# A scheduler's table of matmul durations is changed, and with it the order of 7,588 TensorE instructions

## The chip, the cores and the metric

One core of a Trainium2 chip runs the whole program. The time is device microseconds (us) of one execution. The kernel before took 1705.38, 1706.32 and 1707.93 us in three runs; the median is 1706.32 us. The profile is of one more execution, with a span of 1705.8 us from the first to the last instruction.

## The reference

Two transformer blocks on 512 tokens of width 1024, all in float32:

```python
h = h + hybrid_mixer(rmsnorm(h, mix_norm), ...)           # state-space scan, causal conv, multi-scale pool
h = h + memory_cross_attention(rmsnorm(h, xattn_norm), rmsnorm(mem, mem_norm), ...)
h = h + swiglu(rmsnorm(h, ffn_norm), ...)
x = rmsnorm(h, final_norm)
# layer A
u, qm, gate = split_cols(x @ a_w_in, A_SIZES)             # u: 2 x 1536 channels
y_mix = conformer_conv(u, conv_w, conv_b, g, b)           # a * sigmoid(gl), 31 taps, layer norm, silu
y = concatenate([y_mix, mem_cross_attention(qm, mem_n, w_mkv)]) * silu(gate)
x = layer_norm(ALPHA * x + y @ w_out, pg, pb)
# layer B: the same frame with dsa_attention (12 heads, top-k keys by an index) in place of the conv
```

## The kernel before

**Layout and products.** Activations lie as tiles of 128 channels by 512 tokens. Each weight block (128 x 1024, 512 KB) comes by one DMA into a tile `raw`; ScalarE (ACT) rounds it to a high part `whi` and VectorE (DVE) takes the rest as `wlo` (`prep`, lines 445 to 455). Activations are split the same way. A product is then three matmuls of the short float type (`mm3`, line 457): high by high, high by low, low by high. The first two need only `whi`; the third needs `wlo`. A `dense` unit for one output tile is 8 x 3 = 24 matmuls of 512 columns into one PSUM bank of the group `mm`, of which there are three. A bank is opened by a unit's first matmul and is free again when DVE or ACT has read it. There are also two banks `A`, two `B` and one `C`.

**Order of the work.** The functions do not issue instructions. Every call is recorded (`Program.rec`, line 137) with its engine, its dependencies and an estimated duration `o.dur`. `Program.order` (line 233) then plays a list schedule with these durations, the latencies between engines of a table, and the slots of tiles and banks, and takes for each free engine the ready instruction of the smallest priority. `Program.emit` (line 359) does this once by program order and up to 12 times more (`FBI`) with priorities from a backward pass (`latest`, line 196), keeps the order with the shortest planned end, and issues all instructions in it. So each engine's queue is fixed at build time: on the chip an instruction waits behind all that stand ahead of it on its engine. All instructions carry the line 378 of `emit`; one tells them apart by tiles.

**Layer A, which the prediction speaks of most.** `conv_tile(j)`, j = 0 to 11 (lines 1134 to 1162), makes the gate half with 24 matmuls of `a_gl` (tanh on ACT), then the other half with 24 of `a_a`; one DVE instruction writes their product into the padded tile `pad` (line 1141). Of the 31 taps ACT and GpSimd (POOL) do 11 into an `act` tile, TensorE does one into a bank `B` (a matmul in full float32, tiles `pad,act`, line 1156), and DVE does 19 more on that bank, one `SCALAR_TENSOR_TENSOR B<-pad,vec,B` each (line 1160). A last DVE addition joins the two sums and `lnc.add` collects the layer norm's statistics. Woven between the conv tiles (line 1203) are the memory attention (`score`, `trans`, `out`, with `emit_y` on DVE after it), the 16 gate tiles (24 matmuls each), and `out_tile`s over the four memory heads. After the twelve tiles come `k_proj` for layer B (line 1206: four units of 24 matmuls of 256 columns), `lnc.finish` (line 1207: 4 + 4 statistics matmuls of one column on `C`, a power on POOL, two broadcasts from `ident,rn` and `ident,rq`), and for each of 12 tiles: two DVE instructions, silu on ACT, the product with the gate on POOL, a split on ACT and DVE (lines 1208 to 1213), whose results the eight `out_tile`s over 12 row tiles read (line 1216).

Of the kernel before, what the change touches and what calls it, by code (L numbers as in the profile page):

```python
# [18 lines left out]
T = 512  # L19
# [11 lines left out]
SSD = 600  # L31
# [27 lines left out]
class View:  # L59
    """a lazily resolved access pattern of a tile"""  # L60
# [61 lines left out]
class Program:  # L122
    """records instructions in program order, then orders each engine's by a list schedule"""
# [13 lines left out]
    def rec(s, eng, fn, m, args, kw):  # L137
        o = Op()
# [25 lines left out]
        n = int(np.prod(out.shape[1:]))  # L164
        if eng == "PE":
            one = m == "transpose" or args[1].base.dt == F32R
            o.table = n > 8
            o.dur = n / 2.4 * 2 if m == "transpose" else max(107, n / 2.4) + 2.5 if one else max(27, n / 2.4) * 4
        elif eng == "ACT":
            ptr = sum(isinstance(kw.get(k), View) for k in ("scale", "bias", "accum_out"))  # L170
            o.dur = n * 0.833 + 93 + 93 * ptr - 40 * (isinstance(args[1], View) and args[1].base.psum)
            o.table = _TABLE.get(args[2])
        elif eng == "DVE":
            two = m in ("tensor_tensor", "scalar_tensor_tensor")
            psum = any(x.psum for x in o.tiles)
            wide = [x for x in ins if int(np.prod(x.shape[1:])) > 1]
            ptr = len(ins) - len(wide)
            if m == "reciprocal":
                o.dur = n * 8.3 + 60
            elif m in ("tensor_reduce", "max", "match_replace"):  # L180
                o.dur = int(np.prod(wide[-1].shape[1:])) * 1.042 + 68
            elif not two and not psum:
                o.dur, o.port = n * 0.521 + 68 + 61 * ptr, n > 8
            else:
                o.dur = n * 1.042 + 68 + 61 * min(ptr, 1)
                o.port = two and sum(not x.base.psum for x in wide) == 2 and n > 8
        elif eng == "POOL":
            o.dur, o.port = (958 if kw.get("op") == ALU.pow else n * (2.2 if len(ins) > 1 else 1.0) + 99), n > 8
        else:
            o.dur = n * int(out.shape[0]) * 4 / 360.0  # L190
# [5 lines left out]
    def latest(s, prio):  # L196
        """latest starts, from a list schedule of the reversed program"""
# [8 lines left out]
        while events:  # L206
# [4 lines left out]
            for e, q in ready.items():  # L211
                if busy[e] > now or not q:
                    continue
                o = ops[q[0][1]]
# [18 lines left out]
    def order(s, prio, window):  # L233
# [3 lines left out]
        left, first, last = {}, {}, {}  # L237
# [5 lines left out]
        # slots in use if the rest ran in program order: a tile may take one early only if this never exceeds the number there is  # L243
# [8 lines left out]
        early, wait, back = [], [], deque()  # L252
# [9 lines left out]
        while len(seq) < len(ops):  # L262
# [5 lines left out]
            while fin and fin[0][0] <= now:  # L268
                o = ops[heapq.heappop(fin)[1]]
# [10 lines left out]
            while back and back[0][0] <= now:  # L280
                x = back.popleft()[1]
# [99 lines left out]
def body(ctx, tc, t, out):  # L381
# [141 lines left out]
    class LN:  # L523
        """layer norm over tiles that come one by one, centred first by the mean of the first npil tiles, whose sum is then 0"""
# [29 lines left out]
        def finish(s):  # L554
            """broadcast rows r, q with norm = centred * r - q"""
# [36 lines left out]
    # ================= block 1, mixer =================  # L592
# [27 lines left out]
    # time steps of all heads  # L620
# [30 lines left out]
    # softplus(x) = max(x, 0) + log1p(exp(-|x|)), log1p(e) = 2 atanh(e / (2 + e))  # L651
# [20 lines left out]
    # cumulated steps as rows of heads  # L672
# [16 lines left out]
    # causal convolution of xs, B, C; order of the channel tiles: B0 B1 C0 C1, then xs  # L689
# [15 lines left out]
    # z gate  # L705
# [7 lines left out]
    # B in token rows, B C products  # L713
# [85 lines left out]
    # multi-scale pool  # L799
# [58 lines left out]
    # keys and values of the first memory  # L858
# [76 lines left out]
    # normalised SSD branch  # L935
# [12 lines left out]
    # ================= block 1, cross attention =================  # L948
# [3 lines left out]
    class XAttn:  # L952
        """two heads (2 pr, 2 pr + 1) of 4; q: nd tiles [dims, T] per head; scale(tb): a number or a column per token"""
# [57 lines left out]
    def weave(*lists):  # L1011
        """emits the lists of steps in turns, each spread evenly over the longest"""
        n = max(len(x) for x in lists)
        pos = [0] * len(lists)
        for i in range(n):
            for k, x in enumerate(lists):
                want = -(-(i + 1) * len(x) // n)
                while pos[k] < want:
                    x[pos[k]]()
                    pos[k] += 1  # L1020
# [9 lines left out]
    q = []  # L1030
# [23 lines left out]
    # ================= block 1, swiglu =================  # L1054
# [25 lines left out]
    # taps of layer A: sigmoid(x) = (1 + tanh(x / 2)) / 2, and the half goes to the taps; some as diagonal matrices  # L1080
# [40 lines left out]
    # ================= final norm of block 1 =================  # L1121
# [8 lines left out]
    # ================= block 2, layer A =================  # L1130
# [40 lines left out]
    def gate_tile(w, j, half=False):  # L1171
        """silu(gate); with half, twice that from tanh"""
# [14 lines left out]
    def out_tile(w, j, part, first, ln=None):  # L1187
        """part: the operands by row tile"""
# [37 lines left out]
    # ================= block 2, layer B =================  # L1226
# [103 lines left out]
    # token rows for the last layer norm  # L1330
# [50 lines left out]
    # last projection, token rows  # L1381
# [152 lines left out]
```

## Time and profile before

| | |
|---|---|
| timed runs | 1705.38, 1706.32, 1707.93 us; median 1706.32 |
| the profiled execution's own time | span 1705.8 us (0.5 us under the median; no other time of it is shown) |
| TensorE (PE) | 1665.2 us busy, 98%, 7966 records |
| VectorE (DVE) | 1142.2 us, 67% |
| ScalarE (ACT) | 775.9 us, 45% |
| GpSimd (POOL) | 421.0 us, 25% |
| DMA | mean 92 GB/s |

PE's busy time counts a matmul until its result is out, about 0.39 us for one of 512 columns, while the next starts long before; so the start-to-start spacing tells what a matmul costs in a dense row. A matmul in full float32 shows as two records, a transpose as one: 6912 short-float matmuls, 378 in full float32 and 298 transposes make the 7966 records. The 40 slices of the page show where PE is not full.

### The profile page before, as it was taken

How to read it: one execution, taken by the hardware profiler on the slowest of the kernel's cores; microseconds unless marked ns; L12 is line 12 of the kernel's file. 1: busy time of each engine (PE TensorE's matmuls, PEld its weight loads, DVE VectorE, ACT ScalarE, POOL GpSimd, SP SyncE). 2: the span in 40 equal slices, each digit the busy share in tenths (PEclk: the TensorE clock that was granted, in tenths of full speed). 3: DMA queues.
4: the chain of work that ended last, by engine and by line, in shares of the span. 5: the costliest groups of instructions: out<-in, count | busy, mean ns of one | idle time of the engine just before them, and what ended most of it. 6: DMA issues, size and time to landing. Idle time of an engine off the chain costs nothing. (4 is left out here: it accounts for less than half of the span.)

```text
span 1705.8 us, 21241 instructions
## 1 busy us (share of the span) xinstructions
PE 1665.2 (98%) x7966; PEld 1361.4 (80%) x7966; DVE 1142.2 (67%) x1801; ACT 775.9 (45%) x1349; POOL 421.0 (25%) x325
## 2 busy tenths in 40 slices
PE   9999999999999999999999997999899999999998
PEld 7888678888888888888878775778787788788886
DVE  7836778574565435544477999988747895467754
ACT  6722444444553222332356766545435434545541
POOL 1004433020031001201233678965630000000000
PEclk9999999999999999999999998999999999999999
DMA  7321212531242333322323311232233123211121
GB/s 242 117 86 56 93 50 87 160 99 50 75 131 93 98 99 99 95 79 90 117 91 108 102 56 50 81 127 87 75 124 115 62 99 94 80 63 50 53 84 50
DMA packets 49719, 156.32 MB, mean 92 GB/s; under 512 B 5648, under 2 KB 7568, under 8 KB 49616
## 3 DMA queue, kind: packets, MB, share of 16 engines
q1 hardware_dynamic: 49616, 154.96, 28.2%
q8 instruction: 63, 1.03, 0.3%
q14 instruction: 40, 0.33, 0.1%
HBM read 152.71 MB, written 2.10 MB: 91 GB/s over the span
## 5 line engine op out<-in xcount | busy, mean ns | idle before, releaser
L378 PE MATMUL mm<-act,whi 128*128 128x512 f32 (+1 forms) x3888 | 1194.3, 388 | 18.5 <-DVE act L378 12.9
L378 PEld LDWEIGHTS mm<-act,whi 128*128 128x128 f32 x3888 | 717.8, 189 | 174.3 <-ACT act L378 15.3
L378 PE MATMUL mm<-act,wlo 128*128 128x512 f32 (+1 forms) x1944 | 749.4, 388 | 9.8 <-DVE wlo L378 9.6
L378 ACT ACTIVATE whi<-raw 128x1024 fp32r<-128x1024 f32 (+3 forms) x293 | 289.4, 991 | 582.0 <-PE mm L378 352.5
L378 POOL TENSOR_TENSOR act<-act,act 128x512 f32<-128x512 f32 (+1 forms) x252 | 372.5, 1493 | 683.7 <-DVE act L378 314.8
L378 DVE TENSOR_TENSOR wlo<-raw,whi 128x1024 fp32r<-128x1024 f32 (+3 forms) x293 | 373.2, 1281 | 123.7 <-ACT whi L378 118.9
L378 PEld LDWEIGHTS mm<-act,wlo 128*128 128x128 f32 x1944 | 366.9, 189 | 85.5 <-DVE wlo L378 11.3
L378 DVE TENSOR_TENSOR act<-mm,act 128x512 f32<-128x512 f32 (+3 forms) x173 | 114.6, 664 | 244.9 <-PE mm L378 236.9
L378 ACT ACTIVATE act<-act 128x512 f32<-128x512 f32 (+2 forms) x222 | 134.7, 617 | 104.6 <-DVE act L378 65.9
L378 DVE SCALAR_TENSOR_TENSOR B<-pad,vec,B 128x512 f32<-128x512 f32 x228 | 167.2, 753 | 5.7 <-PE B L378 1.5
L378 DVE TENSOR_TENSOR act<-act,act 128x512 f32<-128x512 f32 (+3 forms) x203 | 138.3, 711 | 26.2 <-ACT act L378 25.3
L378 POOL TENSOR_TENSOR fr<-fv,mhalf 128x1 f32<-128x1 f32 x4 | 2.2, 547 | 410.5 <-DVE fv L378 410.5
L378 ACT ACTIVATE act<-pad,vec 128x512 f32<-128x512 f32 x144 | 94.8, 730 | 11.6 <-DVE pad L378 11.4
L378 PE MATMUL A<-act,act 128*128 128x256 f32 (+6 forms) x488 | 97.8, 342 | 0.3
L378 PEld LDWEIGHTS A<-act,act 128*128 128x128 f32 (+1 forms) x488 | 72.1, 189 | 16.7 <-issue 5.6
L378 PE MATMUL mm<-whi,act 128*128 128x512 f32 x264 | 85.0, 393 | 0.0
L378 ACT ACTIVATE act<-C 128x128 f32<-128x128 f32 (+4 forms) x164 | 52.2, 359 | 70.6 <-PE C L378 68.3
L378 PE MATMUL B<-act,act 128*128 128x128 f32 (+2 forms) x492 | 71.0, 284 | 0.0
L378 PEld LDWEIGHTS B<-act,act 128*128 128x128 f32 (+1 forms) x492 | 61.7, 167 | 9.6 <-issue 3.4
L378 ACT ACTIVATE act<-mm 128x512 f32<-128x512 f32 (+3 forms) x92 | 51.7, 566 | 18.4 <-PE mm L378 18.3
L378 PEld LDWEIGHTS mm<-whi,act 128*128 128x128 f32 x264 | 49.4, 188 | 9.6
L378 PE MATMUL mm<-wlo,act 128*128 128x512 f32 x132 | 51.8, 393 | 0.0
(130 smaller groups left out, 965.6 us busy)
## 6 DMA issues: line engine op xcount, KB each, us to landing
raw<-in_w_g_dram SPq DMA_DIRECT2D x22, 512.0 KB, 3.3
raw<-in_w_u_dram SPq DMA_DIRECT2D x22, 512.0 KB, 3.3
raw<-in_w_om_dram SPq DMA_DIRECT2D x16, 512.0 KB, 3.8
raw<-in_w_d_dram SPq DMA_DIRECT2D x16, 512.0 KB, 3.5
raw<-in_a_gate_dram SPq DMA_DIRECT2D x16, 512.0 KB, 3.4
raw<-in_b_gate_dram SPq DMA_DIRECT2D x16, 512.0 KB, 3.3
raw<-in_b_wo_dram SPq DMA_DIRECT2D x16, 512.0 KB, 3.3
raw<-in_w_xbc_dram SPq DMA_DIRECT2D x12, 512.0 KB, 4.2
```

What stands on the lines that cost most here:

```text
L378: r = o.fn(*[real(a) for a in o.args], **{k: real(v) for k, v in o.kw.items()})
```

## The change

The expression for the planned duration of a PE instruction is another one. `n` is the number of columns, `one` a short-float matmul; the last case is full float32.

```diff
-            o.dur = n / 2.4 * 2 if m == "transpose" else max(107, n / 2.4) + 2.5 if one else max(27, n / 2.4) * 4
+            o.dur = 108.0 if m == "transpose" else max(112.0, n / 2.4 + 14) if one else 2 * max(111.0, n / 1.2 + 2)
```

In ns: a short-float matmul of 512 columns goes from 215.8 to 227.3, of 256 from 109.5 to 120.7; a transpose of 128 from 106.7 to 108; a full float32 matmul of 512 from 853 to 857, of 128 from 213 to 222, of one column from 108 to 222. The rest of the diff takes comments and docstrings out. The instructions, their operands and the number of tiles and banks are the same; the order that `order` and `latest` make of them is not. ACT's function tables, which follow from its order, are loaded 9 times in place of 11. Three places of the new order follow; numbers in names are buffer numbers and differ between the two programs.

**Place 1: conv tile 8, PE and DVE.** The row of PE just ahead of the first low-part matmul of conv tile 8's gate half (the last row of each piece), before:

```order
L378 MATMUL A_8359<-act_8012,act_7315 128x512
L378 MATMUL mm_8369<-act_6810,whi_8313 128x512
L378 MATMUL B_8371<-pad_7986,act_4671 128x512
L378 MATMUL mm_8369<-act_6827,whi_8313 128x512
L378 MATMUL mm_8382<-act_8052,whi_8341 128x512
L378 MATMUL mm_8382<-act_8114,whi_8341 128x512
L378 MATMUL A_8359<-act_8015,act_7658 128x512
L378 MATMUL A_8393<-act_8017,act_7315 128x512
L378 MATMUL A_8393<-act_8022,act_7658 128x512
L378 MATMUL mm_8336<-act_6810,wlo_8439 128x512
```

and after:

```order
L378 MATMUL mm_8339<-act_8078,whi_8200 128x512
L378 MATMUL mm_8346<-act_8024,whi_8282 128x512
L378 MATMUL mm_8346<-act_8078,whi_8282 128x512
L378 MATMUL C_8382<-ident,act_7672 128x128 x4
L378 MATMUL C_8403<-ident,act_7726 128x128 x4
L378 MATMUL C_8416<-ident,act_8008 128x128 x4
L378 MATMUL A_8426<-act_8370,act_7186 128x512
L378 MATMUL A_8426<-act_8372,act_7447 128x512
L378 MATMUL A_8445<-act_8376,act_7186 128x512
L378 MATMUL A_8445<-act_8378,act_7447 128x512
L378 MATMUL mm_8308<-act_6808,wlo_8456 128x512
```

From the end of conv tile 7's second half to that row stand 11 short-float matmuls of 512, 5 full float32 ones and 4 transposes before, and 8, 7 and 14 after. On DVE the low part that this row reads, `wlo_8439`, follows these instructions before:

```order
L378 SCALAR_TENSOR_TENSOR B_8261<-pad_7775,vec_73,B_8261 128x512
L378 SCALAR_TENSOR_TENSOR B_8371<-pad_7986,vec_73,B_8371 128x512
L378 SCALAR_TENSOR_TENSOR B_8261<-pad_7775,vec_73,B_8261 128x512
L378 SCALAR_TENSOR_TENSOR B_8371<-pad_7986,vec_73,B_8371 128x512
L378 TENSOR_TENSOR wlo_8439<-raw_8153,whi_8233 128x1024
L378 TENSOR_TENSOR wlo_8441<-raw_8248,whi_8313 128x1024
```

and after, as `wlo_8456`:

```order
L378 TENSOR_TENSOR act_8211<-act_8211,B_8214 128x512
L378 SCALAR_TENSOR_TENSOR B_8331<-pad_7975,vec_73,B_8331 128x512
L378 SCALAR_TENSOR_TENSOR act_8440<-A_8313,act_7723 128x512
L378 SCALAR_TENSOR_TENSOR B_8331<-pad_7975,vec_73,B_8331 128x512
L378 SCALAR_TENSOR_TENSOR act_8448<-A_8426,act_7998 128x512
L378 SCALAR_TENSOR_TENSOR B_8331<-pad_7975,vec_73,B_8331 128x512 x2
L378 TENSOR_TENSOR wlo_8456<-raw_8116,whi_8179 128x1024
```

Between the instruction that writes conv tile 7's `pad` and this low part, DVE has 20 instructions before and 30 after: 25 taps in place of 19, two joins and two `emit_y` more.

**Place 2: the last two conv tiles, DVE.** From the `pad` of conv tile 10 (first row) to the `pad` of tile 11, before:

```order
L378 SCALAR_TENSOR_TENSOR pad_8470<-act_9025,mm_8972 128x512
L378 TENSOR_TENSOR wlo_9072<-raw_8995,whi_9058 128x1024
L378 SCALAR_TENSOR_TENSOR B_9077<-pad_8470,vec_73,B_9077 128x512 x11
L378 TENSOR_TENSOR act_8750<-act_8750,B_8767 128x512
L378 SCALAR_TENSOR_TENSOR B_9077<-pad_8470,vec_73,B_9077 128x512 x8
L378 TENSOR_TENSOR wlo_9224<-raw_9032,whi_9123 128x1024
L378 TENSOR_TENSOR wlo_9232<-raw_9044,whi_9167 128x1024
L378 TENSOR_TENSOR wlo_9241<-raw_9083,whi_9206 128x1024
L378 SCALAR_TENSOR_TENSOR pad_8592<-act_9131,mm_9140 128x512
```

and after, with the rows behind it:

```order
L378 SCALAR_TENSOR_TENSOR pad_8434<-act_9055,mm_9063 128x512
L378 TENSOR_TENSOR wlo_9119<-raw_9021,whi_9108 128x1024
L378 SCALAR_TENSOR_TENSOR B_9121<-pad_8434,vec_73,B_9121 128x512 x12
L378 TENSOR_TENSOR wlo_9212<-raw_9079,whi_9189 128x1024
L378 SCALAR_TENSOR_TENSOR pad_8526<-act_9172,mm_9169 128x512
L378 SCALAR_TENSOR_TENSOR B_9121<-pad_8434,vec_73,B_9121 128x512
L378 TENSOR_TENSOR wlo_9234<-raw_9088,whi_9214 128x1024
L378 SCALAR_TENSOR_TENSOR B_9232<-pad_8526,vec_73,B_9232 128x512
L378 SCALAR_TENSOR_TENSOR B_9121<-pad_8434,vec_73,B_9121 128x512
L378 SCALAR_TENSOR_TENSOR B_9232<-pad_8526,vec_73,B_9232 128x512
```

Tile 11's `pad` comes after 14 instructions in place of 24, and the taps of both tiles then alternate. On PE the short-float matmuls of 512 columns, those of gate tiles above all, are shared out in another way: from the first low-part matmul of tile 8 to the last matmul of tile 10 stand 312 in place of 283, from there to the first statistics matmul 175 in place of 240, and behind it up to the next norm's statistics 387 in place of 352.

**Place 3: PE where the layer norm of 1536 channels ends.** The second group of statistics (first row) and what follows up to the broadcasts, before:

```order
L378 MATMUL C_9517<-ones,act_8762 128x1 x4
L378 MATMUL mm_9515<-act_6810,wlo_9454 128x512
L378 MATMUL mm_9515<-act_6831,whi_9397 128x512
L378 MATMUL mm_9515<-act_6844,whi_9397 128x512
L378 MATMUL mm_9515<-act_6831,wlo_9454 128x512
L378 MATMUL mm_9515<-act_6839,whi_9397 128x512
```

and after:

```order
L378 MATMUL C_9466<-ones,act_8702 128x1 x4
L378 MATMUL mm_9440<-act_6874,wlo_9413 128x512
L378 MATMUL mm_9440<-act_6890,whi_9312 128x512
L378 MATMUL mm_9440<-act_6896,whi_9312 128x512
L378 MATMUL mm_9440<-act_6890,wlo_9413 128x512
L378 MATMUL mm_9440<-act_6894,whi_9312 128x512
```

`mm_9515` was the eleventh of the plain gate tiles, with one more to come; `mm_9440` is the ninth, with three more to come. From the second broadcast to the first matmul of the eight `out_tile`s stand 33 gate matmuls and 80 of `k_proj` before (all of three units and the start of the fourth), 70 and 55 after (two units and the start of the third).

## Rows read from the trace of the kernel before

**Rows 1.** The page: its first line, the engines' busy time, and PE's busy share in 40 slices, in tenths.

```profile
span 1705.8 us, 21241 instructions
...
PE 1665.2 (98%) x7966; PEld 1361.4 (80%) x7966; DVE 1142.2 (67%) x1801; ACT 775.9 (45%) x1349; POOL 421.0 (25%) x325
...
PE   9999999999999999999999997999899999999998
...
```

**Rows 2.** Busy time by stage: stretch and its length in us, then busy us (records) of PE, PE's weight loads, DVE, ACT, POOL, the granted clock, DMA share, GB/s. The cuts are: 860.3 the broadcast after block 1's last norm; 1030.6 the last matmul of conv tile 7; 1047.7 the first low-part matmul of conv tile 8; 1122.5 the last matmul of conv tile 10; 1178.7 the first statistics matmul of layer A's conv norm; 1284.8 that of the norm after `out_tile`.

```profile
0.00:45.00 45.00, 42.19 (x191) 33.10 (x191) 32.98 (x61) 27.36 (x41) 6.90 (x8) 1.00 0.68 234
45.00:860.30 815.30, 812.38 (x3881) 668.54 (x3880) 467.02 (x622) 320.69 (x500) 145.93 (x129) 1.00 0.30 94
860.30:1030.60 170.30, 166.80 (x763) 133.39 (x763) 152.61 (x213) 113.33 (x213) 94.49 (x73) 1.00 0.25 83
1030.60:1047.70 17.10, 7.74 (x27) 4.15 (x25) 16.99 (x27) 10.80 (x21) 16.62 (x15) 0.81 0.00 0
1047.70:1122.50 74.80, 70.41 (x290) 55.07 (x291) 71.18 (x89) 37.92 (x56) 60.69 (x43) 0.98 0.33 105
1122.50:1178.70 56.20, 56.20 (x246) 45.77 (x245) 48.86 (x55) 29.82 (x44) 42.55 (x30) 1.00 0.33 107
1178.70:1284.80 106.10, 98.88 (x484) 82.95 (x483) 68.67 (x85) 45.77 (x66) 50.60 (x24) 0.97 0.29 92
```

**Rows 3.** Rows that give PE's spacings. From the chain of waits, start, us, what: 108 matmuls of 512 columns in one row. From PE's timeline (start, us, engine, operation, tiles and shapes, count): rows of `k_proj`, 256 columns, three matmuls apart, and six records of the full float32 `out` matmuls.

```profile
1664.94 24.49 PE mm L378 x108
```

```profile
1199.08 0.40 PE L378 MATMUL mm<-act,whi 128*128 128x256 f32 x2
...
1200.16 0.40 PE L378 MATMUL mm<-act,whi 128*128 128x256 f32 x2
```

**Rows 4.** PE's timeline at conv tile 8; in brackets PE's idle time before the row and what ended it.

```profile
1030.62 0.39 PE L378 MATMUL mm<-act,wlo 128*128 128x512 f32 x1
...
1035.71 2.74 PE L378 MATMUL A<-act,act 128*128 128x512 f32 x6
1047.68 0.79 PE L378 MATMUL mm<-act,wlo 128*128 128x512 f32 x1 [9.23 <-DVE wlo L378]
```

**Rows 5.** DVE's timeline in the same stretch.

```profile
1032.48 0.69 DVE L378 SCALAR_TENSOR_TENSOR pad<-act,mm 128x512 f32<-128x512 f32 x1
...
1034.54 11.96 DVE L378 SCALAR_TENSOR_TENSOR B<-pad,vec,B 128x512 f32<-128x512 f32 x18
1046.41 2.96 DVE L378 TENSOR_TENSOR wlo<-raw,whi 128x1024 fp32r<-128x1024 f32 x3
```

**Rows 6.** Busy time and granted clock (the column after POOL's) just behind the two long waits of PE.

```profile
1047.70:1051.40 3.70, 3.70 (x9) 2.93 (x10) 3.70 (x6) 0.63 (x1) 3.62 (x2) 0.51 0.47 131
1207.70:1211.80 4.10, 4.09 (x15) 3.71 (x16) 4.10 (x5) 1.29 (x3) 4.10 (x4) 0.50 0.41 125
```

**Rows 7.** PE's waits from conv tile 8 to tile 10.

```profile
1067.47 1.12 PE L378 MATMUL C<-act,ones 128*128 128x512 f32 x2 [0.56 <-POOL act L378]
1069.31 0.50 PE L378 MATMUL mm<-act,whi 128*128 128x512 f32 x1 [0.72 <-DVE act L378]
1071.45 0.70 PE L378 MATMUL mm<-act,whi 128*128 128x512 f32 x2 [0.47 <-ACT whi L378]
1099.11 0.70 PE L378 MATMUL mm<-act,whi 128*128 128x512 f32 x2 [1.54 <-DVE act L378]
1102.31 0.73 PE L378 MATMUL mm<-act,whi 128*128 128x512 f32 x2 [0.42 <-ACT whi L378]
1112.13 0.73 PE L378 MATMUL mm<-act,whi 128*128 128x512 f32 x2 [0.69 <-ACT act L378]
```

**Rows 8.** DVE's timeline from tile 10's `pad` to the last statistics additions.

```profile
1122.97 0.69 DVE L378 SCALAR_TENSOR_TENSOR pad<-act,mm 128x512 f32<-128x512 f32 x1 [2.29 <-PE mm L378]
...
1125.56 8.67 DVE L378 SCALAR_TENSOR_TENSOR B<-pad,vec,B 128x512 f32<-128x512 f32 x11 [0.57 <-PE B L378]
...
1140.94 5.82 DVE L378 TENSOR_TENSOR wlo<-raw,whi 128x1024 fp32r<-128x1024 f32 x3
1148.96 0.69 DVE L378 SCALAR_TENSOR_TENSOR pad<-act,mm 128x512 f32<-128x512 f32 x1 [2.20 <-PE mm L378]
...
1176.40 1.29 DVE L378 TENSOR_TENSOR act<-act,act 128x512 f32<-128x512 f32 x2
```

**Rows 9.** PE's timeline from the second statistics group through the start of the `out_tile`s.

```profile
1179.82 0.95 PE L378 MATMUL C<-ones,act 128*128 128x1 f32 x8
...
1207.70 0.76 PE L378 MATMUL mm<-act,whi 128*128 128x256 f32 x2 [5.94 <-DVE act L378]
...
1221.20 0.50 PE L378 MATMUL mm<-act,whi 128*128 128x512 f32 x1 [1.21 <-DVE act L378]
```

**Rows 10.** POOL's first gate product and DVE's timeline in the same stretch.

```profile
1189.35 15.12 POOL L378 TENSOR_TENSOR act<-act,act 128x512 f32<-128x512 f32 x1 [6.88 <-ACT act L378]
```

```profile
1185.39 10.93 DVE L378 TENSOR_TENSOR act<-act,act 128x512 f32<-128x512 f32 x18 [2.73 <-ACT act L378]
...
1207.15 1.07 DVE L378 TENSOR_TENSOR act<-mm,act 128x256 fp32r<-128x256 f32 x3
```

**Rows 11.** PE's waits at the first conv tile.

```profile
870.94 0.50 PE L378 MATMUL mm<-act,whi 128*128 128x512 f32 x1 [0.95 <-DVE act L378]
...
874.45 0.73 PE L378 MATMUL mm<-act,whi 128*128 128x512 f32 x2 [1.41 <-ACT act L378]
```

## The prediction, made before the changed kernel ran

> **What bounds the kernel now.** I read the page first: PE is busy for 1665.2 us of 1705.8, and only a few of its 40 slices are under 9 tenths [rows 1]. Since a busy PE need not be a dense one, I took the spacing next: 108 matmuls of 512 columns in 24.49 us are 226.8 ns each [rows 3]. The sum of such spacings is the same in any order, so what an order can change is only where PE stands still (1705.8 - 1665.2 = 40.6 us in all) or runs slowly. The table by stage shows where that is [rows 2]: before 860 us PE idles for 2.8 us at the start and 2.9 us after it; from 860.3 to 1284.8 us, layer A, the idle time is 3.5 + 9.4 + 4.4 + 0 + 7.2 = 24.5 us. Two waits make most of it: 9.23 us for the low part of conv tile 8's weights [rows 4] and 5.94 us in `k_proj` for a bank that DVE has not read yet [rows 9]. [...] In layer A the second engine is DVE: busy for 16.99 of 17.1 us and 71.18 of 74.8 us in the two stages in the middle [rows 2]. So I ask of every move whether PE's or DVE's queue is the later one.
>
> **The table itself.** The new entries are the ones that the trace supports: 227.3 ns planned for 512 columns against 226.8 [rows 3], 120.7 for 256 against 1.08 us for nine, 120 ns [rows 3]. That makes the planner's picture of PE truer, by 5% in the dense parts. It doesn't make any instruction shorter, and the time follows from the places where the two queues cross. [...]
>
> **Stage by stage, against the span of 1705.8 us.** A stage's new length is its PE work by the new order plus what PE then waits. The counts are of the two orders, at 0.227 us a short-float matmul of 512 columns; a full float32 one of 512 is two records, of which six take 2.74 us with the pipeline's end, some 0.86 us a pair [rows 4]; for a transpose I take 0.11 us, an estimate a little under the 0.12 of 256 columns [rows 3].
>
> 860.3 to 1030.6. Up to conv tile 7's end the new order has 3 short-float matmuls more, 2 full float32 ones and 10 transposes less: 0.7 - 1.7 - 1.1 - 0.2 (two of 256 columns) = -2.3 us. Against it, the two waits at the first conv tile (0.95 and 1.41 us [rows 11]) hang on a DVE and ACT chain of splits which the new order serves up to 2 us later against about 1 us more work of `k_proj`, and conv tile 1 opens a bank sooner behind its last reader. I take +1.3, between 0 and +4. Sum -1.0 (-2.3 to +1.7).
>
> 1030.6 to 1047.7, place 1. DVE writes `pad` at 1032.48, starts the low part at 1046.41 and does 18 alternating taps in 11.96 us between, 0.66 us each [rows 5]; PE goes on at 1047.68 [rows 4]. Ten instructions more ahead of it are 6.6 us; `pad` itself comes some 0.5 us sooner against PE. PE's added work there (two full float32 and ten transposes more, three short ones less) is 2.1 us, and lies inside the wait, as do the two banks that the new rows wait for. The stage gets 17.1 + 6.1 = 23.2 us long: +6.1 (+4 to +7).
>
> 1047.7 to 1122.5. PE has 29 matmuls more, +6.6 us. Before, 74.8 us hold 283 x 0.227 + 3 x 0.86 = 66.8 us of work, so 8.0 are lost: 4.4 in six waits [rows 7], 1.9 at the low clock [rows 6], the rest in starts. After the longer wait PE runs later against DVE, which covers those of the six that wait for DVE and POOL. Walking down both queues from the low part on, I find three new near misses: a bank opened within a microsecond of its evacuation (1.1 and 0.5 us) and tile 9's low part (1.5 us), 3.1 in all; with the low clock and starts 5.9. So 73.4 + 5.9 = 79.3 to 79.6: +4.8 (+1.5 to +8).
>
> 1122.5 to 1179.8 (the second statistics group [rows 9]), place 2. PE has 65 matmuls less. Before, its work fills the stretch to the last tenth [rows 2], and DVE has slack: it waits 2.29 and 2.20 us for tile 10's and tile 11's second halves [rows 8]. After, DVE decides. From tile 10's `pad` to the last statistics addition: 25 taps that run alone, 8.67/11 = 0.79 us each, 19.7; 13 that alternate, 0.66 each, 8.6; 8 low parts at 1.77 us, 14.2 (between 1.94, three in 5.82 [rows 8], and 0.99, three in 2.96 [rows 5], and nearer the first because it is from this stretch); two `pad`s, two joins and the two additions, 4.0. That is 46.5, less 0.6 for ends that overlap, plus 0.45 from PE's last matmul to `pad` (1122.5 to 1122.97): 46.4 us where it was 57.3. PE's 175 matmuls and the rest fill 43.2 of them. So -11.0 (-13 to -8).
>
> 1179.8 to 1284.8, place 3. PE has 32 matmuls more here, counted from the second group: 102.2 us of work where there were 94.9. Before, 10.1 us were lost: 5.94 and 1.21 [rows 9], 2.1 at the low clock [rows 6], the rest in starts. The long wait comes from a chain: 18 of the 24 normalising additions on DVE take 10.93 us from 1185.39, during which POOL's first gate product lasts 15.12 us, and only then do the splits and `k_proj`'s evacuations (three at 1207.15) follow [rows 10]. From the second broadcast to the first `out_tile` PE now has 70 x 0.227 + 55 x 0.12 = 22.5 us of work, up to about 1208 if the additions began at 1185.39 as before; DVE needs 24 x 0.61 and three low parts of up to 1.2, some 18 us, after which POOL's product ends and ACT and DVE split it, at about 1206; the first `k_proj` bank is read right behind it. So the wait is covered, and there remain short ones for the later splits, POOL giving one product each 1.7 us: I take 3.0 us lost (1 to 8). 105.2 against 105.0: +0.2 (-2 to +5).
>
> Elsewhere PE keeps the same neighbours or is dense on both sides; statistics broadcasts with a microsecond less work ahead stand against nothing: 0 (-2 to +3).
>
> Sum: -1.0 + 6.1 + 4.8 - 11.0 + 0.2 = -0.9, a span of 1704.9 us; the median stood 0.5 over the span, so **1705.4 us**. The work that left the stretch before the statistics has only moved to both sides of it, and what the covered wait in `k_proj` gives, conv tile 8 takes.
>
> **Rivals.** *Faster.* The order keeps the 11 us and pays less for them: the lost time behind tile 8 falls from 8.0 to about 3, because PE is now the later queue there (for it: it has 6.6 us more work; against it: three banks `mm` are few), the first stage keeps all of its -2.3, and the last loses 1 us instead of 3. That is -0.9 - 2.9 - 1.3 - 2.0 = -7.1: about 1699 us. *Slower.* The wait in `k_proj` stays. The mechanism is DVE's queue behind the broadcast: if the additions and low parts hold POOL's first product longer than PE's 22.5 us of work, the first split, and the bank evacuations queued behind it on DVE, come late, PE stands still as it did for 5.94 us [rows 9] and loses 2.1 at the low clock [rows 6] while the longer wait at tile 8 is paid in full. Then -0.9 + 5.9 + 2.1 - 1.0 (of the 3.0 that are in the sum) = +6.1: 1712 us. For it: the 15.12 us that POOL needed before [rows 10]; against it: three low parts fewer stand in DVE's way. It decides from about 23 us between the second broadcast and the first split on. *The trace corrects the plan everywhere* (many small gains, since an order planned with true spacings fits better) would show in the dense parts, and these have nothing to give: 2.9 us of idle in the 815 us before 860 [rows 2].
>
> **How the numbers follow.** A difference of 0.2%, 3.4 us, is about what can be told from no change. My case, with terms that err by 2 to 3 us each, lies in 1702.5 to 1709: chance 0.42. The faster side, whose terms are the looser ones, 0.36; the slower 0.22. The range reaches into both, from 1698 to 1711.5 us.
>
> **What would show it.** In the changed profile: PE's longest wait is at conv tile 8, before a `mm<-act,wlo` row, released by DVE `wlo`, 13 to 14 us long (step wrong if under 10); no wait of 6 us at a 256-column row; the first statistics of layer A's conv norm start 1 to 4 us earlier than 1178.7 and PE waits some 3 us for them; DVE's second-last and last tiles' taps alternate. The forecast fails if tile 8's wait is no longer than before, or if a new wait over 4 us stands anywhere before 860 us.

## The result: slower, 1721.88 us, and the profile after

The changed kernel took 1714.32, 1714.66, 1721.88, 1722.04 and 1724.95 us, median 1721.88; the kernel before took 1706.29 us beside it. The ratio is 1.0075 (95% interval 1.0053 to 1.0097): slower by 0.75%. The forecast of 1705.4 us was wrong, and so was its range, which ended at 1711.5. The profiled execution is the slowest of the five, with a span of 1723.1 us, 17.3 more than before. The page's first line and its busy times, as in [rows 1]:

```profile
span 1723.1 us, 21234 instructions
...
PE 1676.0 (97%) x7966; PEld 1366.1 (79%) x7966; DVE 1153.7 (67%) x1801; ACT 772.1 (45%) x1347; POOL 407.8 (24%) x325
```

The matmuls are the same 7966 records. PE's idle time has grown from 40.6 to 47.1 us, and the rest of the 17.3 us lies in its busy time, where the clock was lower for longer (its mean is 0.986, and 0.992 before). The table by stage, with the columns of [rows 2] and cut at the same instructions of the program, shows where:

```profile
0.00:45.00 45.00, 41.68 (x181) 32.78 (x182) 32.61 (x63) 27.52 (x41) 7.39 (x8) 0.92 0.67 232
45.00:863.70 818.70, 815.28 (x3893) 670.56 (x3892) 471.11 (x621) 317.85 (x498) 145.64 (x129) 1.00 0.29 94
863.70:1036.30 172.60, 167.03 (x751) 132.96 (x750) 151.97 (x212) 110.16 (x200) 92.11 (x73) 0.99 0.24 80
1036.30:1059.30 23.00, 14.20 (x38) 6.70 (x36) 22.96 (x35) 13.66 (x34) 22.57 (x21) 0.78 0.00 0
1059.30:1144.80 85.50, 77.75 (x319) 60.86 (x320) 74.78 (x83) 39.73 (x58) 64.26 (x43) 0.96 0.34 113
1144.80:1186.30 41.50, 41.50 (x181) 33.30 (x179) 40.19 (x51) 25.74 (x38) 33.52 (x24) 1.00 0.23 76
1186.30:1301.50 115.20, 107.19 (x518) 89.82 (x518) 76.15 (x88) 47.36 (x69) 39.08 (x24) 0.96 0.29 97
```

Cut as in the prediction, with the second statistics group (1179.8 before, 1188.2 after) between the last two:

| stage | before, us | forecast | after, us | measured |
|---|---|---|---|---|
| up to the broadcast at 860.3 | 860.3 | 0 | 863.7 | +3.3 |
| to the end of conv tile 7 | 170.3 | -1.0 | 172.6 | +2.3 |
| to tile 8's first low-part matmul | 17.1 | +6.1 | 23.0 | +5.9 |
| to the last matmul of tile 10 | 74.8 | +4.8 | 85.5 | +10.7 |
| to the second statistics group | 57.4 | -11.0 | 43.5 | -13.9 |
| to the next norm's statistics | 105.0 | +0.2 | 113.3 | +8.3 |
| to the end | 420.9 | 0 | 421.6 | +0.7 |

Two long waits of PE, with the lower clock behind them (0.52 and 0.50), are the largest part of what was not forecast. The first is at conv tile 9. PE's row with its wait, then DVE's and GpSimd's rows of the same moment:

```profile
1099.25 0.80 PE L378 MATMUL mm<-act,wlo 128*128 128x512 f32 x1 [6.24 <-DVE wlo L378]
...
1091.26 7.93 DVE L378 TENSOR_TENSOR wlo<-raw,whi 128x1024 fp32r<-128x1024 f32 x1
...
1083.17 14.94 POOL L378 TENSOR_TENSOR act<-act,act 128x512 f32<-128x512 f32 x12
```

Three low parts of this size took 5.82 us in [rows 8]; this one alone took 7.93. GpSimd's row of products (12 of them from 1083.17) runs without a pause to 1098.11, and the low part ends 1.08 us later, at 1099.19. Behind the wait stands a granted clock of 0.52 (the column after POOL's), and behind the second long wait one of 0.50:

```profile
1099.30:1104.50 5.20, 5.20 (x13) 4.09 (x14) 5.02 (x8) 1.58 (x2) 0.17 (x1) 0.52 0.28 101
1221.50:1227.20 5.70, 4.67 (x16) 3.98 (x17) 5.19 (x7) 5.70 (x11) 3.13 (x2) 0.50 0.18 64
```

The second is in `k_proj`, at a 256-column row, where [rows 9] had 5.94 us. GpSimd's first gate product, DVE's first 16 normalising additions, the reading of the gate tile's bank on ACT, and PE:

```profile
1195.73 1.43 POOL L378 TENSOR_TENSOR act<-act,act 128x512 f32<-128x512 f32 x1 [4.89 <-ACT act L378]
...
1192.92 16.31 DVE L378 TENSOR_TENSOR act<-act,act 128x512 f32<-128x512 f32 x16
...
1220.10 0.81 ACT L378 ACTIVATE act<-act,vec 128x512 f32<-128x512 f32 x1 [2.08 <-DVE act L378]
1220.82 0.58 ACT L378 ACTIVATE act<-mm 128x512 f32<-128x512 f32 x1
...
1221.45 0.80 PE L378 MATMUL mm<-act,whi 128*128 128x256 f32 x2 [6.66 <-ACT act L378]
```

Before, 18 additions took 10.93 us and the first product 15.12 [rows 10]; now the product takes 1.43 us, and each addition 1.02 on average. ACT's silus wait for the additions, the bank of the last gate tile is read behind one of them at 1220.82, and PE, which opens that bank again, goes on at 1221.45.

### The profile page after: what moved, and what is told of

The parts are those of the page before. It is cut to its first block, busy times and chain, and to the rows that moved or that the text cites. A ratio compares the mean times of both kernels' runs of the same rounds, so it can differ in the third digit from the quotient of the medians.

```text
span 1723.1 us, 21234 instructions
## 1 busy us (share of the span) xinstructions
PE 1676.0 (97%) x7966; PEld 1366.1 (79%) x7966; DVE 1153.7 (67%) x1801; ACT 772.1 (45%) x1347; POOL 407.8 (24%) x325
## 4 chain that ended last, share of the span: by engine, by line
PE 84%; DVE 11%; ACT 2%; issue 2%; DMA 1%; SPq 0%; DVEq 0%; POOLq 0%; POOL 0%; ACTq 0%
PE mm L378 73%; PE A L378 4%; DVE B L378 4%; DVE act L378 4%; PE B L378 4%; PE C L378 3%; DVE wlo L378 2%; ACT act L378 1%; ACT whi L378 1%; DVE xm L378 0%; DMA raw<-in_w_xbc_dram 0%; DMA raw<-in_a_wo_dram 0%; DVE pad L378 0%; SPq L378 0%; DVEq L1530 0%
## 5 line engine op out<-in xcount | busy, mean ns | idle before, releaser
L378 POOL TENSOR_TENSOR act<-act,act 128x512 f32<-128x512 f32 (+1 forms) x252 | 359.3, 1438 | 674.3 <-DVE act L378 336.7
L378 DVE TENSOR_TENSOR wlo<-raw,whi 128x1024 fp32r<-128x1024 f32 (+3 forms) x293 | 378.6, 1296 | 144.3 <-ACT whi L378 138.0
L378 DVE TENSOR_TENSOR act<-act,act 128x512 f32<-128x512 f32 (+3 forms) x203 | 146.3, 749 | 22.4 <-ACT act L378 21.3
L378 PE MATMUL A<-act,act 128*128 128x256 f32 (+6 forms) x488 | 101.3, 348 | 0.9 <-ACT act L378 0.9
L378 PEld LDWEIGHTS A<-act,act 128*128 128x128 f32 (+1 forms) x488 | 73.4, 190 | 21.2 <-ACT act L378 6.6
L378 PE MATMUL C<-ident,act 128*128 128x128 f32 (+1 forms) x288 | 50.4, 281 | 7.8 <-ACT act L378 7.2
```

Source lines behind the costliest of these rows:

```text
L378: r = o.fn(*[real(a) for a in o.args], **{k: real(v) for k, v in o.kw.items()})
```

## The experiments

The main theory after the result: DVE and GpSimd hold each other up, the plan has that only instruction by instruction, and on the chip whole rows win or lose (the low part of 7.93 us at tile 9, the product of 15.12 us in [rows 10]). Its rival: true PE durations harm, since too short ones gave DVE and ACT a lead.

### The changed kernel once more

No edit.

> The changed kernel once more, to see a second execution of it: its five times lie on two levels, 1714.3 to 1714.7 and 1721.9 to 1725.0 us. Theory A (single meetings of DVE and POOL that the plan does not contain): the levels differ at one place, conv tile 9, where in the profile after the low part takes 7.93 us on DVE while POOL works 12 products in a row without a pause, PE waits 6.24 us for it and then runs at the lower clock. An execution at the lower level would show that low part in under 2.4 us and no PE wait over 2 us there; one at the upper level shows the 7.9 us again. Rival: the levels differ by many small things (clock, transfers), and the low part takes the same time in both.

Measured: four times of 1719.43 to 1724.57 us, span of the profiled one 1721.5. The low part at tile 9 was quick:

```profile
1090.73 1.78 DVE L378 TENSOR_TENSOR wlo<-raw,whi 128x1024 fp32r<-128x1024 f32 x1
...
1073.65 33.59 POOL L378 TENSOR_TENSOR act<-act,act 128x512 f32<-128x512 f32 x23 [3.34 <-ACT act L378]
...
1102.26 0.50 PE L378 MATMUL mm<-act,wlo 128*128 128x512 f32 x1 [2.98 <-DVE wlo L378]
1217.10 0.80 PE L378 MATMUL mm<-act,whi 128*128 128x256 f32 x2 [6.64 <-ACT act L378]
```

In the same order, at the same place, GpSimd's row now let the low part in, and the lower clock behind it was gone: the matmuls of 512 columns there start 0.23 us apart, where the first profile has 0.43 behind the wait. By the start times of the same matmuls in both traces that was worth some 8.5 us at first. A wait of 2.98 us for the second half's low part and the slower row behind it (0.43 us apart) took 4.6 back, and 1.3 had been lost behind tile 8 (1058.4 to 1061.8 us), so the stage became 2.7 us shorter than in the first profile (82.8 us). Another 2.8 us were lost from the `out_tile`s on, whose matmuls of 512 columns start 0.43 us apart up to 1225.3 us. So the low part explains the place, but "one place makes the two levels" does not hold; what makes them stays open. The `k_proj` wait is there again, 6.64 us.

### Four other orders

Half of the new table each, more refinements with the new table, and the second-best order of the old table:

```diff
# short_only
-            o.dur = 108.0 if m == "transpose" else max(112.0, n / 2.4 + 14) if one else 2 * max(111.0, n / 1.2 + 2)
+            o.dur = n / 2.4 * 2 if m == "transpose" else max(112.0, n / 2.4 + 14) if one else max(27, n / 2.4) * 4
# others_only
+            o.dur = 108.0 if m == "transpose" else max(107, n / 2.4) + 2.5 if one else 2 * max(111.0, n / 1.2 + 2)
# more_tries
-SWITCH, FBI, LATE, REUSE, MIX = 40000, 12, 850, 160, 0.5
+SWITCH, FBI, LATE, REUSE, MIX = 40000, 26, 850, 160, 0.5
# old_second, in the kernel before
-            if r[1] < best[1]:
+            if it == 7:
```

> Only the entry for short-float matmuls is the new one; transposes and full float32 keep the old entries. Theory A (chance of the order): another order, whose time is drawn from the same spread as the others, 1700 to 1725 us, and has its own named waits; planned end by the new table 1688 us against 1686 of the changed kernel and 1684 of the order before, so no better than 1706. Theory B (the longer planned matmuls take away a lead of DVE and ACT before PE): this entry carries the lead, so 1714 to 1725 us, as the changed kernel.

> Only transposes and full float32 matmuls get the new entries; the short-float ones keep the old. Theory A: again an order of its own, 1700 to 1725 us, and not bound to the time before; planned end by the new table 1689 us, the worst of the four. Theory B: the lead is kept, so 1703 to 1709 us, as before.

> The new table, but the planner goes through 26 refinements in place of 12 and takes the order with the shortest planned end, which is now the last: 1683.6 us planned in place of 1685.7. Theory A: the time follows what the plan leaves out and not the 2 us of plan, so anywhere from 1700 to 1725 us; at place 3 the wait before the last unit of k_proj need not come back. Theory B: 1714 us or more, since the table is the same. A third view (the search was cut short, the plan is right): 2 us under the changed kernel's lower level, about 1712 us.

> The old table, but with the order of the eighth refinement in place of the seventh: its planned end is 1601.7 us, 0.6 us over that of the order taken before. Theory A (each order is a draw, and the table matters only in that it draws again): 1712 to 1738 us, as with the four other orders so far, with long waits of its own. Theory B (short planned matmuls give DVE and ScalarE a lead that serves the chip): 1703 to 1710 us, since the lead is the same.

| order | planned end, new table | median, us | ratio (95%) |
|---|---|---|---|
| before | 1684 | 1706.29 to 1707.98 | |
| old_second | not on record | 1726.33 | 1.0112 (1.0097 to 1.0127) |
| others_only | 1689 | 1721.77 | 1.0078 (1.0059 to 1.0097) |
| changed kernel | 1685.7 | 1721.88 | 1.0075 (1.0053 to 1.0097) |
| short_only | 1688 | 1734.05 | 1.0149 (1.0132 to 1.0166) |
| more_tries | 1683.6 | 1738.29 | 1.0174 (1.0156 to 1.0192) |

(The planned ends are the planner's own, for orders of another table replayed by its rules with the new durations; by the old table old_second ends 0.6 us behind the order before.) The lead is not the cause: others_only keeps the old entries where the lead would lie and is as slow as the changed kernel, and with the whole old table an order planned within 0.6 us of the one before takes some 19 us more. Nor does the planned end rank them: before and more_tries, planned within 1 us of each other, took times that are 30 us apart. The theory of a drawn order fits, but its range was too narrow: short_only and more_tries lie 9 and 13 us above the 1725 us that it gave as the end.

Each order has long waits of its own. PE waits 7.38 us at 890 and 8.13 us at 1109 us in short_only, 7.29 us at 1033 us in others_only, and 7.31 us in `k_proj` in old_second. In more_tries the tile 9 event comes larger:

```profile
1103.53 0.80 PE L378 MATMUL mm<-act,wlo 128*128 128x512 f32 x1 [15.59 <-DVE wlo L378]
...
1094.21 10.47 DVE L378 TENSOR_TENSOR wlo<-raw,whi 128x512 fp32r<-128x512 f32 x3
...
1074.24 28.68 POOL L378 TENSOR_TENSOR act<-act,act 128x512 f32<-128x512 f32 x23
```

The three low parts start behind 11 taps, and the first then stands until GpSimd's row of 23 products ends at 1102.92. The order before is the best of six; that it was drawn well fits all of them, but six draws don't settle how the spread comes about.

### Who gets in at the layer norm

The edit leaves the order as it is and lets ACT, which is idle or short of work there, copy n columns onto themselves ahead of the first silu, so that GpSimd's first product asks later. (phase_a to phase_c: two copies. early_before instead moves ACT's rounding of a `k_proj` block from just ahead of that silu to just behind it.) Theory P, of phase: how far into one of DVE's additions the product asks decides whether it gets in. In the changed kernel it asked 0.41 us after the start of one and got in, in the kernel before 0.34 us after and was kept out.

```diff
         S.activation(c, c, AF.Silu, bias=vc("a_ln_b", j), scale=vc("a_ln_g", j))
+        if j == 0:
+            o = prog.ops[-1]
+            o.fn = lambda y, x, *a, f=o.fn, **k: (nc.scalar.activation(y[:, :128], x[:, :128], AF.Copy), f(y, x, *a, **k))
```

> The changed kernel with its order untouched; ScalarE copies 128 columns of the first normalised tile onto themselves just ahead of the first silu behind the layer norm of 1536 channels, an estimated 0.3 us in which it was idle. [...] So that product lasts about 15 us where it took 1.43, the 24 additions and their low parts end 7 to 9 us earlier against their start (27.7 us in the profile after), PE's 6.65 us wait before the last unit of k_proj falls under 2 us, the lower clock behind it goes, and the time is 1710 to 1716 us. Rival: GpSimd's products, now begun 15 us later, hold the out_tiles up by as much, and the time stays within 2 us of the changed kernel's 1722. A second rival: the order of access doesn't depend on 0.3 us, and the profile of this place looks as before.

Measured: 1714.23 us (1713.45 to 1715.27), ratio to before 1.0043 where the changed kernel had 1.0075 and 1.0081. DVE, GpSimd and the longest wait left on PE:

```profile
1187.29 9.72 DVE L378 TENSOR_TENSOR act<-act,act 128x512 f32<-128x512 f32 x16
...
1190.46 14.80 POOL L378 TENSOR_TENSOR act<-act,act 128x512 f32<-128x512 f32 x1 [5.22 <-ACT act L1214]
...
1216.30 1.22 PE L378 MATMUL mm<-act,whi 128*128 128x512 f32 x2 [1.11 <-DVE act L378]
```

The 16 additions take 9.72 us in place of 16.31, the first product 14.80 in place of 1.43, and the `k_proj` wait is gone. The stage from the second statistics group is 107.6 us in place of 113.3: an edit that adds 0.34 us to ACT gains 5.7 us here. The profiled executions differ by more, 11.4 us, since tile 9's low part was quick in this one (1.76 us), which the edit does not touch. The other way round, in the kernel before:

> The kernel before with its order untouched and the same edit with 8 columns, an estimated 0.2 us. [...] Rival (phase is no cause): 15 us again, and 1704 to 1709 us.

> The kernel before, order untouched, with 500 columns in place of 8 in the copy ahead of the first silu: an estimated 0.67 us, a whole period of DVE's additions (0.605 us) and 0.07. With 8 columns GpSimd's request came 0.57 us after the start of an addition and was kept out all the same. Theory P with its window narrowed: the three executions in which GpSimd got in had it at 0.41 us, the five in which it was kept out at 0.11, 0.11, 0.15, 0.34 and 0.57. Now it falls at 0.39 to 0.44 us, so GpSimd gets in: first product about 1.4 us, additions beside products 1.8 us, PE's wait of 5.94 us in k_proj 10 us or more, 1711 to 1717 us. Rival: the phase does not decide it (something else in the changed order does), the product takes 15 us again and the time is 1704 to 1709 us.

> The kernel before, order untouched, two copies of 112 columns ahead of the first silu: GpSimd's request is estimated to fall 0.41 us after the start of one of DVE's additions (0.39 to 0.45). In the three executions in which GpSimd got in, it came at 0.411 to 0.415 us; in the seven in which it was kept out, at 0.11, 0.11, 0.16, 0.34, 0.34, 0.39 and 0.58. Theory P (that window, somewhere in 0.39 to 0.58, decides): first product about 1.4 us, PE's 5.94 us wait in k_proj 10 us or more, 1711 to 1717 us. Rival (something else of the changed order lets GpSimd in): about 15 us, 1704 to 1710 us.

> The same with two copies of 135 columns: the request falls 0.45 us after the start of an addition (0.43 to 0.49). Theory P: as in the run before this one, 1.4 us and 1711 to 1717 us. Rival: 15 us, 1704 to 1710 us.

> The same with two copies of 165 columns: the request falls 0.50 us after the start of an addition (0.48 to 0.54). Theory P: GpSimd gets in here too if the window reaches that far (1.4 us, 1711 to 1717 us); if all three of these runs show 15 us, the phase is not what decides, and the theory falls. Rival: 15 us, 1704 to 1710 us.

All five miss the 1711 to 1717 us of theory P: 1706.17, 1709.47, 1708.47, 1706.55 and 1708.06 us, each within 0.12% of the kernel before beside it, and the product took 14.4 to 14.9 us. The theory of phase fell: 0.39, 0.44 and 0.49 us after the start of an addition were all kept out. What stood out was how far DVE's row had come.

> The order before, with one of ScalarE's instructions moved: the rounding of a weight block of k_proj that stands just ahead of the first silu behind the layer norm now stands just behind it. The silu starts as soon as DVE has its first tile done, 0.26 us earlier, and GpSimd's request falls 0.41 us after the start of the fifth addition of DVE's row, which is where it fell in the three executions in which GpSimd got in; in all ten in which it was kept out, it fell on the sixth, seventh or eighth. Theory P2 (how far DVE's row has run decides): first product about 1.4 us, additions beside products 1.8 us, PE's wait in k_proj 10 us or more, 1711 to 1717 us. Rival (something else of the changed order): 15 us, 1704 to 1710 us.

> The changed kernel, order untouched, with 450 columns copied ahead of the first silu in place of 128: GpSimd's request then falls on the sixth addition in place of the fifth, but at the same 0.41 to 0.43 us after its start. Theory P2 (the place in the row decides): kept out, about 15 us, PE's 6.65 us wait in k_proj under 2 us, 1710 to 1716 us. If the 0.41 us decide: 1.4 us and 1719 to 1725 us.

Both as P2 has it. early_before: 1715.59 us, ratio 1.0053 (1.0036 to 1.0070); the order before now has the changed kernel's trouble:

```profile
1182.93 18.57 DVE L383 TENSOR_TENSOR act<-act,act 128x512 f32<-128x512 f32 x18 [2.73 <-ACT act L383]
...
1185.76 1.43 POOL L383 TENSOR_TENSOR act<-act,act 128x512 f32<-128x512 f32 x1 [5.75 <-ACT act L383]
...
1202.69 0.58 PE L383 MATMUL mm<-act,wlo 128*128 128x256 f32 x1 [3.75 <-DVE wlo L383]
1215.05 0.77 PE L383 MATMUL mm<-act,whi 128*128 128x256 f32 x2 [7.47 <-ACT act L383]
```

18 additions take 18.57 us where they took 10.93 [rows 10]. delay2_after: 1714.84 us (1712.44 to 1715.49), product kept out at the old phase:

```profile
1190.35 9.71 DVE L378 TENSOR_TENSOR act<-act,act 128x512 f32<-128x512 f32 x16
...
1193.79 14.52 POOL L378 TENSOR_TENSOR act<-act,act 128x512 f32<-128x512 f32 x1 [5.50 <-ACT act L1214]
```

The two are single profiles, but they turn the outcome round in both orders. Over all profiled executions with the products on GpSimd, from the starts of the first product and of the additions:

| GpSimd asks during | offset into it, us | executions | first product, us |
|---|---|---|---|
| the 5th addition | 0.41 to 0.42 | 5 (after, after_again, more_tries, old_second, early_before) | 1.43 to 1.44 |
| the 6th | 0.16 and 0.42 | 2 (delay_after, delay2_after) | 14.5 to 14.8 |
| the 7th | 0.11 to 0.58 | 5 (before, delay_before, hoist_before, short_only, others_only) | 14.8 to 15.4 |
| the 8th | 0.39 to 0.49 | 4 (delay2_before, phase_a to phase_c) | 14.4 to 14.5 |

The five of the first row ask 2.82 to 2.83 us after DVE's row began, the earliest of the others 3.17 us. So the line lies somewhere between; no run asks earlier than 2.82, and none tells a count of additions from a time.

### Moves in the order before

```diff
# hoist_before
-        for o in best[0]:
+        q = [o.idx for o in best[0]]
+        for move, behind in [([6870, 6898, 6649], 6624)]:
+            q = [k for k in q if k not in move]
+            k = q.index(behind) + 1
+            q[k:k] = move
+        for o in [s.ops[k] for k in q]:
# gate_dve_before; both_before: this, the move above, and ([7683], 7848), ([7741], 7861)
         G.tensor_tensor(c, c, gate[j], op=ALU.mult)
+        prog.ops[-1].fn = nc.vector.tensor_tensor
```

> The order before with three of DVE's instructions moved ahead: the low part that PE waits 9.23 us for at conv tile 8, and the two low parts behind it, stand 14 taps earlier; their high parts have been ready since 1020.6 to 1031.5 us. If PE is the bound behind that place: PE goes on by 1037 to 1038 us instead of 1047.7, the lower clock goes, DVE's taps come 3 us later, and since DVE has 3 to 8 us of slack up to the last statistics, 4 to 8 us remain: 1699 to 1703 us. Rival, and what the planner says (by the new table the planned end falls by 0.3 us only): DVE is the bound up to the statistics, PE meets the same wait a tile later, and the time is 1704 to 1709 us.

Measured: 1711.49 us, ratio 1.0019 (1.0009 to 1.0029): the rival, and a little worse. PE's wait has moved, and ACT and DVE show to what:

```profile
1057.81 1.22 PE L383 MATMUL mm<-act,whi 128*128 128x512 f32 x2 [9.29 <-ACT act L383]
...
1056.12 0.63 ACT L383 ACTIVATE act<-act 128x512 fp32r<-128x512 f32 x1 [12.74 <-DVE act L383]
...
1055.42 0.67 DVE L383 SCALAR_TENSOR_TENSOR act<-A,act 128x512 f32<-128x512 f32 x1
```

PE passes the old place and stands from 1048.5 on for a bank that ACT reads behind a split, which waits for an `emit_y` that stands behind 21 taps on DVE. DVE's queue is what bounds this stretch.

> The kernel before with its order as planned, but the 12 gate products behind the layer norm are issued on VectorE in place of GpSimd, at the same places of the order. [...] Rival: DVE is the bound of this stage, and 12 products more at 0.6 us, 7 us, come before the splits: 1708 to 1713 us.

Measured: 1705.21 us, ratio 0.9989 (0.9979 to 0.9998); the main theory had 1701 to 1705 us.

```profile
1207.28 0.47 PE L378 MATMUL mm<-act,whi 128*128 128x256 f32 x2 [4.41 <-DVE act L378]
```

Without GpSimd's products no instruction of DVE takes over 1.23 us there, where the longest took 1.78 before. PE's wait was 4.41 us in place of 5.94 [rows 9], and the gain about 2 us, at the edge of what can be told: phase_b, whose profile shows this place unchanged, has 0.9989 too.

> The order before with the same three low parts ahead, the 12 gate products behind the layer norm on VectorE, and two of k_proj's bank readings on DVE ahead of the low parts that stand in their way (6 to 8 us earlier). If the three gains add: tile 8 as in the run with the low parts alone, and PE's 4.4 us wait in k_proj gone with its lower clock, but the first out_tile still has to wait for the first split: 2 to 3 us more than that run gains, 1696 to 1701 us. Rival: the out_tiles wait for the splits by what k_proj no longer waits, and the time is that of the run with the low parts alone, within 2 us.

Measured: 1710.56 us, ratio 1.0016 (1.0004 to 1.0027). The `k_proj` wait fell to 2.1 us with no gain left of it, as the rival had it. No version here beats the kernel before by more than can be measured.

## Why the prediction was wrong, step by step

- **The bound and the table.** Right: the same records, a time set by waits and the clock behind them. The 1.9 and 2.1 us for that clock are my estimate, half of the two stretches in [rows 6]; what the profile after shows is a start-to-start spacing of 0.43 us for 512 columns at a granted clock of 0.50 (1099.84 to 1103.68 us), against 0.227 in [rows 3]. That the table acts only through the order that it draws fits the six orders, which are too few to show it.
- **Up to 860.3 and at the end, "0 (-2 to +3)".** +3.3 and +0.7, together over the end. By the start times of the same matmuls 2.0 of the 3.3 us stand in the first 45 us already (1.1 and 1.3 in after_again and delay_after): PE waits 1.15 and 0.81 us between 6.4 and 8.9 us, and the granted clock of the 45 us is 0.92 (0.50 from 8.9 to 15.0) where it was 1.00 [rows 2]. At 204 to 209 us PE meets three waits (1.49 us the longest) where it had two, and the lower clock behind them lasts 6.8 us (0.53 from 207.1 to 213.9) in place of 3.4 (0.52 from 205.0 to 208.4); at 300 us the same matmuls are 2.7 us late. I had compared the orders closely only in layer A.
- **To conv tile 7, -1.0.** +2.3. A wait of 2.13 us at 906.79, for a bank of `mm` that DVE reads late, belongs to the waits that I took at +1.3, "between 0 and +4", and sized too low. The clock of 0.50 from 875.6 to 879.0 us, behind the waits of the first conv tile, has no term in the sum; it costs half of 3.4 us, by the same estimate.
- **Place 1, +6.1.** +5.9. The length and its reason are right: DVE goes from `pad` to the low part in 20.2 us where it took 13.9, and the stage ends with that low part. But there is no one wait of 13 to 14 us, as I had it. PE stands before the transposes (4.38, 1.55 and 0.88 us for ACT's copies from the one bank `C`) and 1.62 us for the low part, and does more of its work between them, at a clock of 0.78.

```profile
1045.53 0.66 PE L378 MATMUL C<-ident,act 128*128 128x128 f32 x4 [4.38 <-ACT act L378]
...
1059.27 0.50 PE L378 MATMUL mm<-act,wlo 128*128 128x512 f32 x1 [1.62 <-DVE wlo L378]
```

- **Tiles 8 to 10, +4.8.** +10.7. The step that failed is the near miss of "tile 9's low part (1.5 us)": it cost 6.24 us and 5.2 us of work at a clock of 0.52. I had priced low parts from 0.99 to 1.94 us; behind an unbroken row of GpSimd's it took 7.93. The second execution, with 1.78, had 82.8 us, still 3.2 over; delay_after, with 1.76, had 80.7. Over the 73.4 us of work that I had counted, these three lose 12.1, 9.4 and 7.3 us, where it was 8.0 before and the faster rival had about 3.
- **Place 2, -11.0.** -13.9. The mis-sized term is the eight low parts at 1.77 us, 14.2 in all: they took 11.6, and DVE's row from tile 10's `pad` to the last statistics addition 42.8 us, not 46.5. So it was done as early as PE's own work, which I had at 43.2 us and which fills 43.4 of 43.4 us. It is not that DVE caught up while PE waited at tile 9: delay_after, without that wait, needs 43.5 us here too. The first statistics start 7.6 us later than 1178.7, where I had them 1 to 4 earlier; that is what the stages before had lost.

```profile
1156.56 1.49 DVE L378 TENSOR_TENSOR wlo<-raw,whi 128x1024 fp32r<-128x1024 f32 x1
...
1182.18 3.45 DVE L378 TENSOR_TENSOR wlo<-raw,whi 128x1024 fp32r<-128x1024 f32 x2
```

- **Place 3, +0.2.** +8.3, the largest miss. The failed step is "so the wait is covered". From the second broadcast (1192.07) to the first split (1221.30) it took 29.2 us, beyond the 23 from which I had the slower rival decide, so that rival is what came, 10 us over its 1712 with the other terms. But its mechanism was turned round: the additions did not hold GpSimd's product up, the products held the additions up. The 0.61 us per addition came from a row in which GpSimd was kept out [rows 10], and I carried it over as if it were the additions' own. delay_after, which restores that, has 107.6 us: 2.4 over my 105.2.

With tile 9's long low part and place 3's slow additions out, the forecast would still have been 6.8 us too low: delay_after, in which the one was quick and GpSimd kept out, has a span of 1711.7 against my 1704.9. Of that, 2.5 us stand before the broadcast and 3.3 from there to tile 7's end.

## What to carry to other kernels

Where two engines shut each other out, a duration read from a trace belongs to who was winning there (0.61 us an addition in [rows 10], 1.02 in the changed kernel); before a sum carries it to another order, ask what the other engine does at that moment, and price both outcomes. A planned order is one of many with nearly equal planned ends: 2 us of plan said nothing about 30 us of time here, so make several and time them. A wait of PE that is moved ahead only pays if the queue behind it, here DVE's, isn't the bound (hoist_before, 1711.49 us).

## What the runs showed of the hardware

DVE's additions of two SBUF tiles and GpSimd's products hold each other up here: in the profile after, an addition that follows another starts 0.60 us later, and 1.70 to 1.72 us later when a product is let in beside it. In the runs the wait can last a whole row of instructions: 15.12 us for a product behind 21 DVE instructions of 0.6 to 1.2 us, up to the first pause in DVE's row (0.52 us at 1203.34), and 7.93 us for a low part behind the rest of a GpSimd row of 1.3 us each. When GpSimd asked during the 5th addition of the row, it got in and the two took turns (5 executions of 5, all 2.82 to 2.83 us after the row began); when it asked from the 6th on, it was kept out to the end of the row (11 of 11). Why the 5th, no run shows.

At tile 9 that does not carry over. Four executions of the same order (after, after_again, delay_after, delay2_after) have DVE ask for the low part 0.60 to 0.61 us into the same product of the same unbroken GpSimd row. Three let it in (1.76 to 1.79 us) and one kept it out (7.93), so there the times in the profile don't tell which it will be.
